# Moving a mixing stage's element work from GpSimd to VectorE, and a new order of its pieces

## The chip, the cores and the metric

The kernel runs on one core of one Trainium2 chip. The metric is the device time of one execution in microseconds (us). Five engines work in parallel, each through its own queue in a fixed order: TensorE (PE, matrix products and transposes), VectorE (DVE), ScalarE (ACT), GpSimd (POOL) and SyncE (SP, which here issues most transfers).

## The reference

Input `x` is 1024 tokens by 1024 features in float32. A first block (four attention branches, merge, output projection) is followed by a second one, and the change is in the second block's mixing. There `z = rms_norm(x) @ w_in` is split into columns for four mixers, whose outputs of 256 features each are joined and multiplied by `w_out`; an MLP and a gated projection follow.

```python
a, b = jnp.split(conf_ab, 2, axis=-1)             # conformer convolution
u = causal_depthwise_conv(a * sigmoid(b), w_dw)   # 31 taps
y_conf = silu(layer_norm(u, ln_g, ln_b)) @ w_pw

c = jnp.cumsum(log_sigmoid(f_logit), axis=1)      # forgetting attention, 4 heads of 64
logits = q @ k.T * scale + c_i - c_j              # causal mask, softmax, @ v

y_sc = sc_b * causal_depthwise_conv(sc_c * sc_h, w_sc)     # short convolution, 3 taps

# multiscale pool: mean of the last 2, 4, 8, 16 tokens, minus the token,
# a 64x64 product for each group, a scale

h = h + rms_norm(concat([y_conf, y_att, y_sc, y_pool]) @ w_out)
```

## The kernel before

All large products keep float32 accuracy by splitting each operand in a high part (rounded to the chip's fp32r type) and a low part (the rest), and by adding three products: high by high, high by low, low by high (`mm3`, lines 229 to 231). A product of 128 by 512 outputs over 1024 inputs is thus 24 matmuls. High parts are made by `copy` (line 147 on ScalarE, 149 on VectorE), low parts by `sub_lo`, which subtracts the high part from the value, on GpSimd (line 155) or on VectorE (line 157):

```python
if eng == "p":
    po.tensor_tensor(lo, x, hi.bitcast(F32), op=ALU.subtract)
else:
    ve.scalar_tensor_tensor(out=lo, in0=x, scalar=scale, in1=hi.bitcast(F32), ...)
```

Weights come from memory in pieces (`wr`) and are split into `wh` and `wl` by `split_w`. Which engine makes a low part is in the table `_T`: `WLO2` for the weights of the mixing stage, `CLO` for the conformer's output, a fixed pattern in `split_mix` for the mixers' outputs. In the kernel before, all of these are GpSimd's (`split_mix`: the first half of the tokens GpSimd's, the second VectorE's). GpSimd also adds the two halves of an attention tile's output in `join` (line 825, used in both blocks), computes the shift adds of the pooling (line 1512) and the power -1/2 of a normalization (line 1447).

The conformer's convolution has 31 taps for two groups of 128 channels (m = 0, 1) and two halves of 512 tokens. Each tap is one VectorE instruction (line 1332) that reads the input shifted by some tokens and adds it, times a weight, to an accumulator. The taps are Python generators in a list `convs`; `conv_steps(n)` lets n taps be written into the program. It is called with `CPP` = 2 after each large product (`product_done`), with `CS` after each attention tile, and to the end by the item `t`.

The order of the mixing stage is the string `WORK` in `_T`: each item is one piece of work, and a framework's list scheduler then orders the instructions of each engine by the program's order, dependences and buffers. `s0` and `s1` are the short convolution's channel groups with their products, `A` one query tile of the first pair of heads (eight), `B` one of the second pair, `q` the second pair's queries and keys, `p` the pooling, `c` one step of the conformer's finish (transposes, layer normalization, product), `w` the weights of the output projection, `0a` to `7` the splits of a mixer's output into parts (`split_mix`), `e` one early product of the output projection, `g` the gains, `t` the rest of the taps.

An attention tile: scores on TensorE (`s`, lines 795 to 799), maximum on VectorE (`Pm`, `mx`, line 836), exponential on ScalarE, scaling on VectorE (line 150), transposes on TensorE (`t`, line 274), their high parts on ScalarE and low parts on VectorE (`PT`), value matmuls (`o`, line 814), `join`.

Of the kernel before, what the change touches and what calls it, by code (L numbers as in the profile page):

```python
# [12 lines left out]
ALU = mybir.AluOpType  # L13
# [4 lines left out]
P = 128  # L18
# [6 lines left out]
SLOPES = [2.0 ** -2, 2.0 ** -4, 2.0 ** -6, 2.0 ** -8]  # L25
QS = 0.125

_T = dict(STA='s', XN1=0, PWT=1, PO='0x1', PO2={}, PS=2, PSX=0, PSE='a', PB=99, PEA=(0, 1, 4), WB=8, XL=3, CLO='p', STE=None, STW=None, ST1='b', ST2='b', PLP='pvv', WLO2='p', QXP=1, LW='vp', LEAD=10, FD={0: 'g', 1: 'b', 6: 'g'}, FW=(0, 2), AG=0, PREO=(0, 2, 1), PMB=0, PWB=1, PM=3, SG=2, FA={(0, 2): 'g', (0, 3): 'mmm', (0, 7): 'qm', (1, 0): 'gg', (1, 6): 'gz'}, FB={(0, 3): 'm', (0, 7): 'qm', (1, 3): 'm', (1, 5): 'z', (1, 7): 'm'}, FC={(0, 3): 'mm', (0, 7): 'q', (1, 3): 'zm', (1, 6): 'm'}, NORM='v', NORM2='v', CS=8, MM=2, SB=2, TB=3, OB=1, WHI='aaav', WLO='pv', PTH='a', NW=9, NBLK=31, PTB=2, XN=1, AS=(2, 4, 6, 7), CPP=2, CALT=1, WORK='s0 A A A A A A A A s1 q t B c B B c c B p w B 5 6b c c c 4 0a 1a g 6a 7 3a 2 e e c c c B e B c B 1b e 0b 3b', KS=(2, 0, 3, 1))


_C1 = [("trel", 1024), ("wrel", 640), ("crel", 256), ("brel", 128), ("brel2", 128), ("dm", 512), ("xi", 256), ("zeta", 256)]
# [45 lines left out]
def hybrid_then_mix_kernel(ctx: ExitStack, tc, I, c1, c2, out, dbg=None, upto=99):  # L77
# [162 lines left out]
    convs = []  # L240

    def conv_steps(n):
        for _ in range(n):
            if convs:
                if next(convs[0], "end") == "end":
                    convs.pop(0)
                elif _T["CALT"]:
                    convs.append(convs.pop(0))

    def product_done(last):  # L250
        conv_steps(_T["CPP"])
# [550 lines left out]
    def pv(dst, Pm, n, lo, v, start=True, stop=True):  # L802

        for c0 in range(0, n, 4):
            w = min(4, n - c0)
            tp = trb()
            for j in range(w):
                transpose(tp[:, j * P:(j + 1) * P], Pm[:, (c0 + j) * P:(c0 + j + 1) * P], ident)
            PT = cur[0].tile([P, 4, 2, P], F32R, name=nm("PT"), tag="PT", bufs=_T["PTB"])
            t3 = tp[:, :w * P].rearrange("p (j q) -> p j q", q=P)  # L810
            copy(PT[:, :w, 0, :], t3, pick("pt", _T["PTH"]))
            sub_lo(PT[:, :w, 1, :], t3, PT[:, :w, 0, :])
            for j in range(w):
                pe.matmul(dst, v(lo + c0 + j), PT[:, j].rearrange("p a q -> p (a q)"), start=start and c0 + j == 0,  # L814
                          stop=stop and c0 + j == n - 1, skip_group_check=True)

    def join(dst, o_):

        u = cur[0].tile([P, P], F32, name=nm("ju"), tag="ju", bufs=2)
        for hh in range(2):  # L820
            r = slice(hh * 64, hh * 64 + 64)
            oh = o_[:, hh * 256:hh * 256 + 256]
            copy(u[r, :], oh[64:128, :P], "a")
            ve.tensor_reduce(out=dst[r, :], in_=oh[0:64, :].rearrange("p (a q) -> p q a", a=2), op=ALU.add, axis=AX.X)  # L824
        po.tensor_tensor(dst, dst, u[:], op=ALU.add)  # L825
# [517 lines left out]
    for m in range(2):  # L1343
        u, w, evac = conf_group(m)
        us.append(u)
        first.append(w)
        conf_evac.append(evac)
        z_half(hT2, w, 0, evac)
        convs.append(conv(m, 0))
    assert not pend  # L1350
    uid[1] = 1
    ph.close()
# [9 lines left out]

    for m in range(2):
        z_half(hT2, first[m], 1, conf_evac[m])
        convs.append(conv(m, 1))
    qk0, w, evac = qk_group(0)
    z_group(hT2, w, evac)
    qk = [qk0]
# [54 lines left out]
    def conf_rest():  # L1423
        wp = W()
        raw = main.tile([P, 2, 256], F32, name=nm("wr"), tag="w", bufs=NW)
        hi, lo = [cur[0].tile([P, 2, 256], F32R, name=nm("wp"), tag="wp", bufs=2) for _ in range(2)]
        sy.dma_start(raw[:], kview(I["w_conf_pw_2"][0]))
        copy(hi[:], raw[:], "a")
        sub_lo(lo[:], raw[:], hi[:], "p")
        wp.hi = lambda k, c0, c1: hi[:, k, c0:c1]  # L1430
        wp.lo = lambda k, c0, c1: lo[:, k, c0:c1]
        sa = A(2)
        for half in range(2):
            sa.alloc(half, 0)
            vv = blk(F32, (P, 2, 512))
            for q in range(4):
# [12 lines left out]
                ve.tensor_scalar(xc[:], tp[:, :256], mv[:, 0:1], r[:, 0:1], op0=ALU.subtract, op1=ALU.mult)  # L1449
                tp = trb()  # L1450
                for m in range(2):
                    transpose(tp[:, m * P:(m + 1) * P], xc[:, m * P:(m + 1) * P], ident)
                for m in range(2):
                    ve.tensor_scalar(vv[:, m, q * P:(q + 1) * P], tp[:, m * P:(m + 1) * P], V["ln_g"][:, m:m + 1],
                                     V["ln_b"][:, m:m + 1], op0=ALU.mult, op1=ALU.add)
                yield
            for m in range(2):
                t = tmp("tz", 512)
                ac.activation(t[:], vv[:, m, :], AF.Tanh, scale=0.5)
                ve.scalar_tensor_tensor(out=vv[:, m, :], in0=t[:], scalar=1.0, in1=vv[:, m, :], op0=ALU.add, op1=ALU.mult)  # L1460
                copy(sa.hi(m, half), vv[:, m, :], "a")
                sub_lo(sa.lo(m, half), vv[:, m, :], sa.hi(m, half), _T["CLO"])
# [10 lines left out]
    def split_mix(k, halves=(0, 1)):  # L1473
        for half in halves:
            mix.alloc(half, k // 2)
            cs = slice(half * 512, (half + 1) * 512)
            copy(mix.hi(k, half), y32[k][:, cs], "a")
            sub_lo(mix.lo(k, half), y32[k][:, cs], mix.hi(k, half), "pv"[half])

    def short_conv(m):  # L1480
        if True:
# [16 lines left out]
    def pooling():  # L1498
# [7 lines left out]
        for m in range(2):  # L1506
# [5 lines left out]
                eng.tensor_tensor(dst[r, l:], src[r, :S - l], src[r, l:], op=ALU.add)  # L1512
                copy(dst[r, :l], src[r, :l], "v")
            s2 = blk()
            shift_add(po, s1, g, 1)
            if m == 0:
                lo_, hi_ = slice(0, 64), slice(64, 128)
                shift_add(po, s2, s1, 2, hi_)
                ve.tensor_copy(s2[lo_, :], s1[lo_, :])
                fin, fre = s2, s1  # L1520
            else:
                lo_, hi_ = slice(0, 64), slice(64, 128)
                shift_add(po, s2, s1, 2)
                shift_add(po, s1, s2, 4)
                shift_add(po, s2, s1, 8, hi_)
# [5 lines left out]
            ve.tensor_sub(fre[:, :16], fre[:, :16], g[:, :16])  # L1531
            for half in range(2):
# [17 lines left out]
    def out_early():  # L1550
        for t in range(NT // 2):
# [6 lines left out]
            ve.tensor_mul(early[t], m[:], gains[0][:, :512])  # L1558
            yield

    steps = dict(A=attention(0), B=attention(1), c=conf_rest(), e=out_early())
    works = dict(g=load_gains, s0=lambda: short_conv(0), s1=lambda: short_conv(1), t=lambda: conv_steps(140), q=second_qk, p=pooling)
    for c in steps:
        works[c] = lambda c=c: next(steps[c])
    for k in range(8):
# [514 lines left out]
```

## Time and profile before

| | us |
|---|---|
| median of 3 runs | 2347.11 (2343.71 to 2349.87) |
| the profiled execution | 2345.36 |
| its span in the profile | 2343.5 |
| TensorE busy | 2239.7 (96%) |
| VectorE busy | 1499.8 (64%) |
| ScalarE busy | 963.1 (41%) |
| GpSimd busy | 600.0 (26%) |

Mean granted clock of TensorE over the profiled execution: 0.983 of the full clock. The mixing stage lies between about 1185 and 1536 us of the span. A profile row names a line, an engine, an operation and tiles (output, an arrow, inputs), with buffer numbers left out; a number behind `x` counts instructions.

### The profile page before, as it was taken

How to read it: one execution, taken by the hardware profiler on the slowest of the kernel's cores; microseconds unless marked ns; L12 is line 12 of the kernel's file. 1: busy time of each engine (PE TensorE's matmuls, PEld its weight loads, DVE VectorE, ACT ScalarE, POOL GpSimd, SP SyncE). 2: the span in 40 equal slices, each digit the busy share in tenths (PEclk: the TensorE clock that was granted, in tenths of full speed). 3: DMA queues.
4: the chain of work that ended last, by engine and by line, in shares of the span. 5: the costliest groups of instructions: out<-in, count | busy, mean ns of one | idle time of the engine just before them, and what ended most of it. 6: DMA issues, size and time to landing. Idle time of an engine off the chain costs nothing. (4 is left out here: it accounts for less than half of the span.)

```text
span 2343.5 us, 30368 instructions
## 1 busy us (share of the span) xinstructions
PE 2239.7 (96%) x11004; PEld 1856.9 (79%) x11004; DVE 1499.8 (64%) x2849; ACT 963.1 (41%) x1937; POOL 600.0 (26%) x514
## 2 busy tenths in 40 slices
PE   7999999999989999999997997899999999999898
PEld 6788888888877778887876886677888878888787
DVE  7634456665667766534589766566567677677773
ACT  6211344444546544422312343534544453344442
POOL 4222110011265533324331125312133430000021
PEclk9999999999999999999998998999999999999999
DMA  9431211122132252224311110146555695534222
GB/s 327 153 95 58 64 63 55 45 91 63 41 122 86 82 155 81 86 81 153 109 42 50 46 59 28 46 171 211 174 180 189 198 357 194 177 108 156 95 74 90
DMA packets 202784, 272.73 MB, mean 116 GB/s; under 512 B 17086, under 2 KB 126214, under 8 KB 202634
## 3 DMA queue, kind: packets, MB, share of 16 engines
q1 hardware_dynamic: 194240, 257.95, 34.1%
q10 hardware_dynamic: 8394, 12.84, 1.8%
q8 instruction: 87, 1.43, 0.2%
q14 instruction: 63, 0.52, 0.1%
HBM read 199.43 MB, written 71.32 MB: 116 GB/s over the span
## 5 line engine op out<-in xcount | busy, mean ns | idle before, releaser
L229 PE MATMUL mm<-blk,wh 128*128 128x512 f32 x1264 | 506.1, 401 | 26.7 <-DVE blk L157 10.5
L230 PE MATMUL mm<-blk,wh 128*128 128x512 f32 x1264 | 502.2, 397 | 0.6 <-DVE blk L157 0.6
L231 PE MATMUL mm<-blk,wl 128*128 128x512 f32 x1264 | 500.8, 396 | 1.0 <-POOL wl L155 1.0
L229 PEld LDWEIGHTS mm<-blk,wh 128*128 128x128 f32 x1264 | 239.1, 189 | 80.6 <-issue 14.2
L231 PEld LDWEIGHTS mm<-blk,wl 128*128 128x128 f32 x1264 | 239.2, 189 | 50.7 <-POOL wl L155 1.4
L155 POOL TENSOR_TENSOR wl<-wr,wh 128x1024 fp32r<-128x1024 f32 (+2 forms) x70 | 172.0, 2457 | 412.3 <-ACT wh L147 192.5
L230 PEld LDWEIGHTS mm<-blk,wh 128*128 128x128 f32 x1264 | 239.6, 190 | 47.0 <-DVE blk L157 1.0
L229 PE MATMUL mm<-wh,blk 128*128 128x512 f32 (+3 forms) x544 | 196.9, 363 | 5.2 <-DVE fl L149 2.1
L231 PE MATMUL mm<-wh,blk 128*128 128x512 f32 (+3 forms) x544 | 193.6, 357 | 1.1 <-DVE blk L157 1.1
L157 DVE SCALAR_TENSOR_TENSOR wh<-blk,wh 128x1024 fp32r<-128x1024 f32 x116 | 138.3, 1221 | 71.6 <-issue 54.2
L147 ACT ACTIVATE wh<-blk 128x1024 fp32r<-128x1024 f32 x116 | 117.1, 1053 | 162.6 <-PE s L1991 75.7
L230 PE MATMUL mm<-wl,blk 128*128 128x512 f32 (+3 forms) x480 | 170.0, 355 | 5.7 <-DVE wl L157 5.0
L307 POOL TENSOR_TENSOR sm<-sm,mhalf 128x1 f32<-128x1 f32 x64 | 38.4, 603 | 444.7 <-DVE sm L306 427.7
L147 ACT ACTIVATE blk<-mm 64x512 fp32r<-64x512 f32 (+3 forms) x138 | 78.1, 569 | 160.4 <-PE mm L231 112.4
L157 DVE SCALAR_TENSOR_TENSOR PT<-t,PT 128x512 fp32r<-128x512 f32 (+3 forms) x224 | 111.3, 515 | 47.6 <-ACT PT L147 46.7
L147 ACT ACTIVATE PT<-t 128x512 fp32r<-128x512 f32 (+3 forms) x224 | 95.2, 460 | 110.7 <-PE o L814 70.4
L147 ACT ACTIVATE wh<-wr 128x1024 fp32r<-128x1024 f32 (+2 forms) x91 | 93.7, 1031 | 98.6 <-DMA wr<-in_w_in_dram 22.5
L229 PEld LDWEIGHTS mm<-wh,blk 128*128 128x128 f32 x544 | 103.4, 190 | 22.6 <-issue 2.3
L231 PEld LDWEIGHTS mm<-wh,blk 128*128 128x128 f32 x544 | 103.4, 190 | 16.9 <-DVE blk L157 1.9
L230 PEld LDWEIGHTS mm<-wl,blk 128*128 128x128 f32 x480 | 91.7, 191 | 19.3 <-DVE wl L157 6.5
L825 POOL TENSOR_TENSOR blk<-blk,ju 128x128 f32<-128x128 f32 x64 | 34.5, 538 | 278.9 <-DVE blk L824 278.8
L1332 DVE SCALAR_TENSOR_TENSOR blk<-blk,dwc,blk 128x512 f32<-128x512 f32 (+23 forms) x124 | 102.6, 878 | 0.4
(364 smaller groups left out, 4912.5 us busy)
## 6 DMA issues: line engine op xcount, KB each, us to landing
acc<-acc SPq DMA_DIRECT2D x96, 256.0 KB, 2.6
wr<-in_w_merge_dram SPq DMA_DIRECT2D x32, 512.0 KB, 4.0
wu<-in_w_up_dram SPq DMA_DIRECT2D x32, 512.0 KB, 5.4
blk<-in_w_down_dram SPq DMA_DIRECT2D x32, 512.0 KB, 7.1
blk<-ss SPq DMA_DIRECT2D x32, 512.0 KB, 3.5
wr<-in_w_in_dram SPq DMA_DIRECT2D x27, 512.0 KB, 4.2
ss<-us SPq DMA_DIRECT2D x48, 256.0 KB, 2.3
blk<-sa SPq DMA_DIRECT2D x24, 512.0 KB, 3.3
```

The source lines that it names most:

```text
L147: return ac.activation(dst, src, AF.Copy, scale=1.0 if scale is None else scale)
L155: po.tensor_tensor(lo, x, hi.bitcast(F32), op=ALU.subtract)
L157: ve.scalar_tensor_tensor(out=lo, in0=x, scalar=scale, in1=hi.bitcast(F32), op0=ALU.mult, op1=ALU.subtract)
L229: pe.matmul(dst, sh, mh, start=(i == 0), stop=False)
L230: pe.matmul(dst, sh, ml, start=False, stop=False)
L231: last = pe.matmul(dst, sl, mh, start=False, stop=(i == n - 1))
L307: po.tensor_tensor(dst, dst, mhalf[:, :m], op=ALU.pow)
L825: po.tensor_tensor(dst, dst, u[:], op=ALU.add)
L1332: ve.scalar_tensor_tensor(out=acc[:, c:c1], in0=u[:, c - l:c1 - l], scalar=w, in1=acc[:, c:c1], op0=ALU.mult, op1=ALU.add)
```

## The change

Low parts of the mixing stage's weights (`WLO2`), of the conformer's output (`CLO`), of its last weight `wp` and of the mixers' outputs go to VectorE, as do the pooling's shift adds and `join`'s add (the last in both blocks). The taps take the two channel groups in turn within one half of the tokens and then the second half; the calls that write them stand in `tc.issue_after`, named after the last matmul of a product or attention tile. The conformer's finish normalizes tile q before it transposes back tile q - 1. The pooling's grouped products become an item of their own (`P`), and `WORK` is new: the pooling and its products of z come ahead of `s1`, the conformer's first half (taps `t`, steps `c`) between the first `B` tiles, its second half (`u`) later.

```diff
-_T = dict(... CLO='p', ... WLO2='p', ... CS=8, ... WORK='s0 A A A A A A A A s1 q t B c B B c c B p w B 5 6b c c c 4 0a 1a g 6a 7 3a 2 e e c c c B e B c B 1b e 0b 3b', ...)
+_T = dict(... CLO='v', ... WLO2='v', ... CS=4, CSB=8, ... WORK='s0 A A A A A A A A p s1 q t c B c B c B c B c 0a 1a P w 5 4 6 7 g 2 3a e u c B e c B c e B c c e B 1b 0b 3b', ...)
...
             if convs:
-                if next(convs[0], "end") == "end":
-                    convs.pop(0)
-                elif _T["CALT"]:
-                    convs.append(convs.pop(0))
+                half, steps_ = convs.pop(0)
+                if next(steps_, "end") != "end":
+                    convs.insert(sum(h == half for h, _ in convs), (half, steps_))
...
     def product_done(last):
-        conv_steps(_T["CPP"])
+        with tc.issue_after(last.ins):
+            conv_steps(_T["CPP"])
...
-                pe.matmul(dst, v(lo + c0 + j), PT[:, j].rearrange("p a q -> p (a q)"), start=start and c0 + j == 0,
+                behind_pe[0] = pe.matmul(dst, v(lo + c0 + j), PT[:, j].rearrange("p a q -> p (a q)"),
...
-        po.tensor_tensor(dst, dst, u[:], op=ALU.add)
+        ve.tensor_tensor(dst, dst, u[:], op=ALU.add)
...
-        sub_lo(lo[:], raw[:], hi[:], "p")
+        sub_lo(lo[:], raw[:], hi[:])
...
+            held = None
+            for q in range(4):
+                xc = normed(q)
+                if held is not None:
+                    turned(q - 1, held)
+                held = xc
                 yield
+            turned(3, held)
...
-            sub_lo(mix.lo(k, half), y32[k][:, cs], mix.hi(k, half), "pv"[half])
+            sub_lo(mix.lo(k, half), y32[k][:, cs], mix.hi(k, half))
...
-            shift_add(po, s1, g, 1)
+            shift_add(ve, s1, g, 1)
...
-        conv_steps(_T["CS"] if n[0] in "A" else 0)
+        if n[0] in "AB":
+            with tc.issue_after(behind_pe[0].ins):
+                conv_steps({"A": _T["CS"], "B": _T["CSB"]}[n[0]])
```

Two places of the order. VectorE's queue near the end of the taps, before (`blk` with two `blk` inputs and `dwc` is a tap, `fl` the forget logits):

```order
L149 CAST wh_11967<-wr_11961 128x1024
L1332 SCALAR_TENSOR_TENSOR blk_11224<-blk_11312,dwc,blk_11224 128x482
L1332 SCALAR_TENSOR_TENSOR blk_11223<-blk_11225,dwc,blk_11223 128x512
L1332 SCALAR_TENSOR_TENSOR blk_11224<-blk_11312,dwc,blk_11224 128x512
L157 SCALAR_TENSOR_TENSOR blk_11676<-mm_11898,blk_11676 128x4x64
L149 COPY fl<-mm_11898 128x4
L1332 SCALAR_TENSOR_TENSOR blk_11223<-blk_11225,dwc,blk_11223 128x512
L1332 SCALAR_TENSOR_TENSOR blk_11224<-blk_11312,dwc,blk_11224 128x512
L1378 TENSOR_TENSOR fl<-fl,bf 128x32
```

And with the change, at the same place:

```order
L1334 SCALAR_TENSOR_TENSOR blk_11223<-blk_11225,dwc,blk_11223 128x512
L1334 SCALAR_TENSOR_TENSOR blk_11224<-blk_11312,dwc,blk_11224 128x512
L157 SCALAR_TENSOR_TENSOR blk_11676<-mm_11898,blk_11676 128x4x64
L149 COPY fl<-mm_11898 128x4
L157 SCALAR_TENSOR_TENSOR wl_11968<-wr_11961,wh_11967 128x1024
L1334 SCALAR_TENSOR_TENSOR blk_11224<-blk_11312,dwc,blk_11224 128x482
L157 SCALAR_TENSOR_TENSOR wl_11972<-wr_11964,wh_11971 128x1024
L1334 SCALAR_TENSOR_TENSOR blk_11223<-blk_11225,dwc,blk_11223 128x512
L1334 SCALAR_TENSOR_TENSOR blk_11224<-blk_11312,dwc,blk_11224 128x512
L1380 TENSOR_TENSOR fl<-fl,bf 128x32
L157 SCALAR_TENSOR_TENSOR wl_12090<-wr_12087,wh_12089 128x1024
```

Three low parts `wl` of 1024 columns have come into the queue between the taps. The taps themselves stand where they stood, ahead of the first attention tile.

TensorE's queue behind the last product of the second pair's queries and keys, before (`mm` with `wh` and `wl` is a large product; `t` are transposes, `s` scores):

```order
L231 MATMUL mm_13041<-blk_11055,wl_12943 128x512
L274 MATMUL t_13138<-c_63,blk_11223 128x128
L274 MATMUL t_13138<-c_63,blk_11224 128x128
L229 MATMUL mm_13356<-blk_10677,wh_13348 128x512
L230 MATMUL mm_13356<-blk_10678,wh_13348 128x512
L231 MATMUL mm_13356<-blk_10677,wl_13349 128x512
L229 MATMUL mm_13356<-blk_10677,wh_13348 128x512
L795 MATMUL s_13203<-blk_12926,blk_12924 128x384
L797 MATMUL s_13203<-blk_12928,blk_12924 128x384
L799 MATMUL s_13203<-causR,identR 128x128
```

And with the change:

```order
L231 MATMUL mm_13164<-blk_11055,wl_13066 128x512
L276 MATMUL t_13246<-c_63,Pm_13225 128x128
L276 MATMUL t_13252<-c_63,Pm_13231 128x128
L276 MATMUL t_13272<-c_63,blk_11223 128x128
L276 MATMUL t_13272<-c_63,blk_11224 128x128
L797 MATMUL s_13362<-blk_13049,blk_13047 128x384
L799 MATMUL s_13362<-blk_13051,blk_13047 128x384
L801 MATMUL s_13362<-causR,identR 128x128
L797 MATMUL s_13368<-blk_13050,blk_13048 128x384
L799 MATMUL s_13368<-blk_13052,blk_13048 128x384
L801 MATMUL s_13368<-causR,identR 128x128
```

Before, the pooling's products of z stand between the tiles here. With the change these stand earlier, and behind the last product of q and k come only tiles' scores, transposes and value matmuls, with the conformer's small products, up to the first early product of the output projection.

## Rows read from the trace of the kernel before

**Rows 1.** The page's first part: busy time of each engine over the span (instructions behind x).

```profile
PE 2239.7 (96%) x11004; PEld 1856.9 (79%) x11004; DVE 1499.8 (64%) x2849; ACT 963.1 (41%) x1937; POOL 600.0 (26%) x514
```

**Rows 2.** Windows of the three stretches; columns named in the first line.

```profile
core 0: us, PE busy (x) PEld busy (x) DVE busy (x) ACT busy (x) POOL busy (x), PEclk, DMA share, GB/s
1185.00:1302.00 117.00, 99.49 (x506) 84.36 (x505) 112.36 (x165) 22.72 (x39) 25.11 (x13) 0.93 0.14 37
1302.00:1413.00 111.00, 110.73 (x574) 92.38 (x573) 75.02 (x172) 48.27 (x108) 30.01 (x21) 1.00 0.20 57
1413.00:1536.00 123.00, 102.00 (x463) 80.01 (x462) 74.09 (x184) 53.14 (x114) 46.51 (x38) 0.88 0.13 39
```

**Rows 3.** TensorE's waits, 1185 to 1302: waited for, us in all, times, longest.

```profile
PE mm L229 <- DVE fl L149: 8.0, 2, 5.9
PE mm L229 <- DVE blk L157: 6.2, 1, 6.2
```

**Rows 4.** A window at low granted clock, columns as in rows 2.

```profile
1449.00:1466.00 17.00, 12.33 (x44) 10.22 (x43) 14.30 (x38) 4.84 (x13) 6.90 (x5) 0.51 0.01 1
```

**Rows 5.** VectorE's groups by shape, 1185 to 1302, and line 1332 (ns min/median/max).

```profile
L1332 DVE SCALAR_TENSOR_TENSOR blk<-blk,dwc,blk 128x512 f32<-128x512 f32 x57 | 46.2, 844 | 0.0
...
L1332 DVE SCALAR_TENSOR_TENSOR blk<-blk,dwc,blk 128x505 f32<-128x505 f32 x2 | 3.6, 1815 | 0.0
...
L1332 DVE SCALAR_TENSOR_TENSOR blk<-blk,dwc,blk 128x492 f32<-128x492 f32 x2 | 2.5, 1249 | 0.0
...
L149 DVE CAST wh<-wr 128x520 fp32r<-128x520 f32 x1 | 0.4, 420 | 0.0
...
L1332 DVE SCALAR_TENSOR_TENSOR blk<-blk,dwc,blk x117: 705/737/2891, 1189.3 to 1301.5; 128x512 f32<-128x512 f32 x57, 128x511 f32<-128x511 f32 x2, 128x510 f32<-128x510 f32 x2, 128x509 f32<-128x509 f32 x2
```

**Rows 6.** Timeline of VectorE, of GpSimd beside it, of VectorE later (start, us).

```profile
1207.64 5.69 DVE L1332 SCALAR_TENSOR_TENSOR blk<-blk,dwc,blk 128x505 f32<-128x505 f32 x2
...
1205.15 7.64 POOL L155 TENSOR_TENSOR wl<-wr,wh 128x1024 fp32r<-128x1024 f32 x2 [6.01 <-issue]
...
1285.58 3.11 DVE L1332 SCALAR_TENSOR_TENSOR blk<-blk,dwc,blk 128x512 f32<-128x512 f32 x2
```

**Rows 7.** GpSimd's groups by shape, 1185 to 1302.

```profile
L155 POOL TENSOR_TENSOR wl<-wr,wh 128x1024 fp32r<-128x1024 f32 x5 | 15.8, 3170 | 31.4 <-DVE wh L149 25.3 <-issue 6.0
L155 POOL TENSOR_TENSOR wl<-wr,wh 128x520 fp32r<-128x520 f32 x4 | 6.0, 1504 | 35.2 <-DMA wr<-in_w_in_dram 27.5 <-DVE wh L149 7.5
```

**Rows 8.** VectorE's groups by shape, 1185 to 1536.

```profile
L157 DVE SCALAR_TENSOR_TENSOR PT<-t,PT 128x512 fp32r<-128x512 f32 x24 | 16.3, 685 | 8.4 <-ACT PT L147 8.3
...
L157 DVE SCALAR_TENSOR_TENSOR blk<-blk,blk 128x512 fp32r<-128x512 f32 x8 | 6.3, 791 | 5.5 <-ACT blk L147 5.5
...
L1528 DVE SCALAR_TENSOR_TENSOR blk<-blk,c,blk 128x1008 f32<-128x1008 f32 x2 | 2.5, 1263 | 0.0
...
L157 DVE SCALAR_TENSOR_TENSOR wl<-wr,wh 128x1024 fp32r<-128x1024 f32 x2 | 2.4, 1223 | 0.1
...
L836 DVE CUSTOM_DVE_ANT_0 Pm<-s,xb 128x128 f32<-128x128 f32 x8 | 2.3, 288 | 4.8 <-DMA xb<-cF_d 3.4 <-PE s L799 1.4
```

**Rows 9.** Windows of the pooling's products and the early ones, as in rows 2.

```profile
1414.40:1436.00 21.60, 21.54 (x109) 18.13 (x109) 13.09 (x38) 6.91 (x20) 5.76 (x5) 1.00 0.08 25
1490.00:1531.00 41.00, 36.19 (x190) 28.67 (x188) 25.83 (x58) 22.00 (x45) 6.58 (x7) 1.00 0.17 52
```

**Rows 10.** VectorE's waits, 1413 to 1536, columns as in rows 3.

```profile
DVE sm L856 <- ACT Pm L848: 7.6, 6, 2.4
DVE Pm L836 <- PE t L274: 7.0, 4, 5.4
...
DVE xc L1449 <- POOL sm L1447: 5.9, 4, 3.2
```

**Rows 11.** GpSimd's instructions on the tile `ju` (ns min/median/max).

```profile
L825 POOL TENSOR_TENSOR blk<-blk,ju x64: 451/460/1952, 304.0 to 1533.3; 128x128 f32<-128x128 f32 x64
```

**Rows 12.** Window in the first block, columns as in rows 2.

```profile
600.00:800.00 200.00, 185.93 (x1058) 158.55 (x1057) 142.21 (x205) 107.48 (x239) 111.73 (x125) 0.98 0.30 94
```

More of the change, by code (lines that the diff above doesn't have):

```diff
@@ L26 @@
 QS = 0.125
-_T = dict(STA='s', XN1=0, PWT=1, PO='0x1', PO2={}, PS=2, PSX=0, PSE='a', PB=99, PEA=(0, 1, 4), WB=8, XL=3, CLO='p', STE=None, STW=None, ST1='b', ST2='b', PLP='pvv', WLO2='p', QXP=1, LW='vp', LEAD=10, FD={0: 'g', 1: 'b', 6: 'g'}, FW=(0, 2), AG=0, PREO=(0, 2, 1), PMB=0, PWB=1, PM=3, SG=2, FA={(0, 2): 'g', (0, 3): 'mmm', (0, 7): 'qm', (1, 0): 'gg', (1, 6): 'gz'}, FB={(0, 3): 'm', (0, 7): 'qm', (1, 3): 'm', (1, 5): 'z', (1, 7): 'm'}, FC={(0, 3): 'mm', (0, 7): 'q', (1, 3): 'zm', (1, 6): 'm'}, NORM='v', NORM2='v', CS=8, MM=2, SB=2, TB=3, OB=1, WHI='aaav', WLO='pv', PTH='a', NW=9, NBLK=31, PTB=2, XN=1, AS=(2, 4, 6, 7), CPP=2, CALT=1, WORK='s0 A A A A A A A A s1 q t B c B B c c B p w B 5 6b c c c 4 0a 1a g 6a 7 3a 2 e e c c c B e B c B 1b e 0b 3b', KS=(2, 0, 3, 1))
+_T = dict(STA='s', XN1=0, PWT=1, PO='0x1', PO2={}, PS=2, PSX=0, PSE='a', PB=99, PEA=(0, 1, 4), WB=8, XL=3, CLO='v', STE=None, STW=None, ST1='b', ST2='b', PLP='pvv', WLO2='v', QXP=1, LW='vp', LEAD=10, FD={0: 'g', 1: 'b', 6: 'g'}, FW=(0, 2), AG=0, PREO=(0, 2, 1), PMB=0, PWB=1, PM=3, SG=2, FA={(0, 2): 'g', (0, 3): 'mmm', (0, 7): 'qm', (1, 0): 'gg', (1, 6): 'gz'}, FB={(0, 3): 'm', (0, 7): 'qm', (1, 3): 'm', (1, 5): 'z', (1, 7): 'm'}, FC={(0, 3): 'mm', (0, 7): 'q', (1, 3): 'zm', (1, 6): 'm'}, NORM='v', NORM2='v', CS=4, CSB=8, MM=2, SB=2, TB=3, OB=1, WHI='aaav', WLO='pv', PTH='a', NW=9, NBLK=31, PTB=2, XN=1, AS=(2, 4, 6, 7), CPP=2, CALT=1, WORK='s0 A A A A A A A A p s1 q t c B c B c B c B c 0a 1a P w 5 4 6 7 g 2 3a e u c B e c B c e B c c e B 1b 0b 3b', KS=(2, 0, 3, 1))
 _C1 = [("trel", 1024), ("wrel", 640), ("crel", 256), ("brel", 128), ("brel2", 128), ("dm", 512), ("xi", 256), ("zeta", 256)]
@@ L244, in conv_steps @@
             if convs:
-                if next(convs[0], "end") == "end":
-                    convs.pop(0)
-                elif _T["CALT"]:
-                    convs.append(convs.pop(0))
+                half, steps_ = convs.pop(0)
+                if next(steps_, "end") != "end":
+                    convs.insert(sum(h == half for h, _ in convs), (half, steps_))
+    behind_pe = [None]
     def product_done(last):
-        conv_steps(_T["CPP"])
+        with tc.issue_after(last.ins):
+            conv_steps(_T["CPP"])
         due = []
@@ L813, in pv @@
             for j in range(w):
-                pe.matmul(dst, v(lo + c0 + j), PT[:, j].rearrange("p a q -> p (a q)"), start=start and c0 + j == 0,
-                          stop=stop and c0 + j == n - 1, skip_group_check=True)
+                behind_pe[0] = pe.matmul(dst, v(lo + c0 + j), PT[:, j].rearrange("p a q -> p (a q)"),
+                                         start=start and c0 + j == 0, stop=stop and c0 + j == n - 1, skip_group_check=True)
     def join(dst, o_):
@@ L1348, in hybrid_then_mix_kernel @@
         z_half(hT2, w, 0, evac)
-        convs.append(conv(m, 0))
+        convs.append((0, conv(m, 0)))
     assert not pend
@@ L1364, in hybrid_then_mix_kernel @@
         z_half(hT2, first[m], 1, conf_evac[m])
-        convs.append(conv(m, 1))
+        convs.append((1, conv(m, 1)))
     qk0, w, evac = qk_group(0)
@@ L1435, in conf_rest, with normed @@
             vv = blk(F32, (P, 2, 512))
-            for q in range(4):
+            def normed(q):
                 t = 4 * half + q
@@ L1449, in conf_rest, with turned @@
                 ve.tensor_scalar(xc[:], tp[:, :256], mv[:, 0:1], r[:, 0:1], op0=ALU.subtract, op1=ALU.mult)
+                return xc
+            def turned(q, xc):
                 tp = trb()
@@ L1514, in pooling @@
             s2 = blk()
-            shift_add(po, s1, g, 1)
+            shift_add(ve, s1, g, 1)
             if m == 0:
                 lo_, hi_ = slice(0, 64), slice(64, 128)
-                shift_add(po, s2, s1, 2, hi_)
+                shift_add(ve, s2, s1, 2, hi_)
                 ve.tensor_copy(s2[lo_, :], s1[lo_, :])
@@ L1522, in pooling @@
                 lo_, hi_ = slice(0, 64), slice(64, 128)
-                shift_add(po, s2, s1, 2)
-                shift_add(po, s1, s2, 4)
-                shift_add(po, s2, s1, 8, hi_)
+                shift_add(ve, s2, s1, 2)
+                shift_add(ve, s1, s2, 4)
+                shift_add(ve, s2, s1, 8, hi_)
                 ve.tensor_copy(s2[lo_, :], s1[lo_, :])
@@ L1531, in pooling, with pool_out @@
             ve.tensor_sub(fre[:, :16], fre[:, :16], g[:, :16])
+            pooled.append((bd, fre, fin))
+    pooled = []
+    def pool_out():
+        for m, (bd, fre, fin) in enumerate(pooled):
             for half in range(2):
@@ L1559, in out_early, with conv_rest @@
             yield
+    def conv_rest(half):
+        while any(h <= half for h, _ in convs):
+            conv_steps(1)
     steps = dict(A=attention(0), B=attention(1), c=conf_rest(), e=out_early())
-    works = dict(g=load_gains, s0=lambda: short_conv(0), s1=lambda: short_conv(1), t=lambda: conv_steps(140), q=second_qk, p=pooling)
+    works = dict(g=load_gains, s0=lambda: short_conv(0), s1=lambda: short_conv(1), t=lambda: conv_rest(0), u=lambda: conv_rest(1), P=lambda: pool_out(), q=second_qk, p=pooling)
     for c in steps:
```

## The prediction

> **What bounds the kernel.** I read the page's first part, then windows over the mixing stage, then what TensorE waits for in each, then single instructions. TensorE is busy for 96% of the span [rows 1], so time can only come from the idle 4% or from stretches at a lower granted clock, and the mixing stage holds a large part of both. I cut it in three [rows 2]. The first stretch, 117 us, ends where the taps end: VectorE is busy 112.4 us of it (96%) and TensorE 99.5, so VectorE sets the pace. In the second, 111 us (second convolution, first-pair tiles A, second-pair q and k), TensorE is busy 110.7 us at full clock. In the third, 123 us (second-pair tiles B, the conformer's finish, the early products), it is busy 102.0 us, at a mean granted clock of 0.88. In the first stretch TensorE waits for VectorE almost alone [rows 3]: 5.9 us at once for the evacuation of the forget logits (`fl`), 6.2 us for a low part. With such gaps the granted clock falls to the 1.2 GHz level, as from 1449 to 1466, where it is 0.51 [rows 4].
>
> **What the moves return on VectorE.** In the first stretch 57 taps of 512 columns have a mean of 844 ns, while the median of all 117 taps is 737 [rows 5]: 57 x 0.107 = 6.1 us too much. Two pairs of other lengths are stretched like that of 505 columns (2 x 1.08 = 2.2 us each), three like that of 492 (2 x 0.51 = 1.0 each). Together 13.5 us. The timeline shows the cause [rows 6]: two taps take 5.69 us instead of 1.47 just while GpSimd runs two `wl` low parts in 7.64. Low parts on GpSimd cost VectorE time; without them I let all 13.5 us go.
>
> **What they add there.** Five `wl` of 1024 columns and four of 520 [rows 7] now run on VectorE. Its own prices are 1.223 us for 1024 columns and 0.685 for 512 [rows 8]: 5 x 1.22 + 4 x 0.69 = 8.9 us. By the order two long and four short ones (5.2 us) stand ahead of the `fl` evacuation, three long ones behind it. Of the 13.5 us, 1.6 lie behind it (two taps in 3.11 us [rows 6]), so it comes 11.9 - 5.2 = 6.7 us earlier. **First stretch: -7 us.** Bounds: if nothing of the stretching goes, +5 us; if both groups of waits on VectorE go whole, -14. I take the middle of the gain, since VectorE is still over 90% busy there. A new wait could come with it: a low part in VectorE's queue waits for the weight's transfer, with taps queued behind it. GpSimd stood idle 27.5 us for that before its short low parts [rows 7], the far bound; but VectorE's own copy of such a weight, in the same place of its queue, waited 0.0 [rows 5]. I take 0.
>
> **What the ties do.** Nothing, by the order: they bind instructions of the engine on which the named instruction runs, which is TensorE, and taps run on VectorE. All of them still stand ahead of the first A tile, as before. The new alternation (both channel groups inside half 0, then half 1) leaves each duration as it was.
>
> **The second stretch.** The pooling's four products of z (96 matmuls) come forward from the third stretch to a place under the A tiles. In the third they took 21.6 us with TensorE busy throughout [rows 9]. Here TensorE has no idle time to lend: +22 here, -22 there, net 0. VectorE gains the six shift adds of the pooling (1.26 us each by the nearest row, 1008 columns [rows 8], 7.6 us), about six `wl` (7.3 us) and the pooling's scaling: with them it is busy some 95 of 133 us, still less than TensorE. I cost them at nothing; without that cover they are 15 us. The transfers of the pooling's weights pass those of q in SP's queue; DMA is busy 0.20 of this stretch [rows 2], so 0.
>
> **The third stretch.** Without the pooling's products 123 - 22 = 101 us are left. Now nothing of 24 matmuls stands behind q and k: up to the first early product the order has score, transpose and value matmuls of five B tiles, the conformer's half 0 and four small grouped products. On TensorE these are 131 matmuls, about 16 us at full clock by their columns (21.6 / 96 = 0.225 us for 512). On VectorE the 106 instructions between q's last low part and the last one that the early products need come to 43.9 us by the unstretched durations of their shapes: low parts of blocks 9.5, of PT 5.2, score maxima 8.3, scaling 4.8, conformer 10.4, reductions and joins 4.0, small ones 1.7. So VectorE sets the pace here. Its use in the nearest stretch of before, 1449 to 1466, with no product either, was 14.3 of 17.0 us, 84% [rows 4]: 43.9 / 0.84 = 52 us; the first low part of the early products stands 7 us sooner, so I take 50. The conformer's transposes of one tile now behind the normalizing of the next spare waits on GpSimd's power (5.9 us before [rows 10]); that lies inside the 84%. Then come the early products with tiles B5 to B7: 219 matmuls, 35 us at full clock by their columns; from 1490 to 1531 TensorE was 88% busy [rows 9], and small matmuls cost more than their columns: 46 us. Sum 96 against 101. **Third stretch: -5 us.** Bounds: VectorE at 100% and a covered tail, 44 + 40 = 84, -17; VectorE at the third stretch's mean use, 74.1 / 123 = 60% [rows 2], 73 + 46 = 119, +18.
>
> **The joins of the first block.** 48 adds of 128x128 go from GpSimd (median 460 ns [rows 11]) to VectorE, where no row has the shape: 0 to 22 us in all. In the least covered stretch there TensorE is 93% and VectorE 71% busy [rows 12]. I take 0, nearest to the lower end since TensorE covers them; without that cover, up to 22.
>
> **Sum.** -7 + 0 - 5 + 0 = -12 us against the profiled execution (2345.36 us, span 2343.5): 2333.4, so 2333. The median of the runs stands 1.75 us above the profiled one, well under the 0.3% (7 us) that a measurement of this kernel can tell.
>
> **The rivals.** (1) *Uncovered second-pair tiles.* From the end of q to the first early product nothing long stands on TensorE. For it: VectorE's waits in the third stretch are for ScalarE's exponentials and TensorE's transposes [rows 10], one chain through three engines, and an idle TensorE falls to 0.5 clock [rows 4]. Against it: two or three tiles and a conformer group are under way at once. It decides once VectorE's use there falls under 70% (63 us). At 60%: +18 - 7 = +11, 2356 us.
>
> (2) *All idle time and half clock of the stage goes:* -10 in the first stretch, -17 in the third: 2318. Against it: VectorE has more to do in all three.
>
> (3) *The first stretch's gain is given back.* The A tiles start sooner, but their first maxima wait for the forget bias that goes through DRAM (3.4 us [rows 8]) and the end of q stays where it was. Only about half of the third's gain is left: 2343.
>
> (4) *The moves cost what they add and return nothing.* If the stretching had another cause, the first stretch would be +5 us, and the third, its low parts at 791 ns instead of 685 [rows 8], 44 x 1.15 / 0.84 = 60 instead of 52, +3: 2353. The taps of rows 6 speak against it. A rule of the Trainium skill speaks for it (Perfetto Trace Analysis, section Optimizing Scalar/DVE Operations): where VectorE is saturated, giving some of its work to GpSimd may pay; the change takes work from GpSimd in just the stretch where VectorE is 96% busy. The same section adds that the two share a read port, so that it might not help; by that half, the trace agrees.
>
> **How the numbers follow.** Forecast 0.50 (its own range 2325 to 2341), (1) 0.19, (2) 0.11, (3) 0.15, (4) 0.05. Faster by over 0.3% (under 2340): 0.46 of the forecast and (2), 0.57. Slower (over 2354): 0.14 of (1) and 0.02 of (4), 0.16. Within: the other 0.27. The range 2319 to 2355 leaves out half of (1), half of (2) and the tail of (4).
>
> **What would show it.** In the profile after: taps near 740 ns without stretched pairs; TensorE's wait for `fl` under 2 us and the taps done about 5 us sooner; no gap of TensorE from the first A tile to the end of q, which comes about 15 us later than before; then some 50 us with VectorE over 80% busy and TensorE half idle, part of it at 0.5 clock; a first block as long as before. I am wrong if that stretch takes over 63 us, or if the taps stay as long as they were.

## The result and the profile after

Over 7 runs each, the changed kernel takes 2336.25 us (2332.15 to 2339.66) and the kernel before 2348.13 (2343.71 to 2351.46): a ratio of 0.9948, 95% interval 0.9933 to 0.9963, or 12 us less. The profiled execution took 2339.66 us, with a span of 2337.8. That is only 5.7 us under the profiled one of before, because its span lost 8.1 us ahead of the mixing stage: 3.7 in the first 400 matmuls and 3.7 in a piece of the first block that comes back below. So I compare stretches, not spans.

The first part of the page of the changed kernel:

```profile
PE 2239.1 (96%) x11004; PEld 1854.8 (79%) x11004; DVE 1519.8 (65%) x2952; ACT 963.0 (41%) x1937; POOL 491.1 (21%) x411
```

GpSimd lost 109 us of work, and VectorE has only 20 more [rows 1]. The windows of [rows 2], by the same work, follow. They begin some 8 us later in the span; the second ends with the second pair's queries and keys; the third is split at the first early product and ends at the place in the work where 1536 lay before. Columns as there:

```profile
1193.00:1310.00 117.00, 107.02 (x542) 90.63 (x541) 111.58 (x180) 24.64 (x41) 3.30 (x4) 0.94 0.16 42
1310.00:1434.00 124.00, 119.73 (x614) 99.92 (x612) 86.51 (x206) 49.91 (x110) 2.45 (x3) 1.00 0.18 53
1434.00:1468.50 34.50, 27.07 (x122) 18.34 (x122) 33.09 (x105) 21.91 (x53) 3.25 (x5) 0.90 0.06 16
1468.50:1528.60 60.10, 53.83 (x266) 43.02 (x267) 37.78 (x86) 28.07 (x58) 5.88 (x4) 0.97 0.21 70
```

In the first, TensorE gets through 542 matmuls in 117 us, against 506. VectorE's groups in that window and TensorE's waits there answer to [rows 5], [rows 7] and [rows 3]:

```profile
L1334 DVE SCALAR_TENSOR_TENSOR blk<-blk,dwc,blk 128x512 f32<-128x512 f32 x60 | 42.7, 746 | 0.3
...
L157 DVE SCALAR_TENSOR_TENSOR wl<-wr,wh 128x1024 fp32r<-128x1024 f32 x6 | 7.3, 1220 | 0.0
...
L157 DVE SCALAR_TENSOR_TENSOR wl<-wr,wh 128x520 fp32r<-128x520 f32 x4 | 2.8, 688 | 0.0
...
L1334 DVE SCALAR_TENSOR_TENSOR blk<-blk,dwc,blk 128x505 f32<-128x505 f32 x2 | 1.5, 737 | 0.0
```

```profile
PE mm L230 <- DVE wl L157: 4.4, 2, 2.9
PE mm L229 <- DVE fl L149: 1.6, 1, 1.6
PE mm L229 <- DVE blk L157: 1.3, 2, 1.1
```

Taps have a mean of 746 ns instead of 844, the stretched pairs are gone (505 columns: 737 instead of 1815), the low parts cost what their prices said. The waits for `fl` and for the low part `blk` fell from 14.2 us to 2.9, and a new one of 4.4 us came, for the short low parts `wl`.

To follow a stretch through all kernels I take four marks with the same work between them in each: the first matmul of the first block's output projection, the first maximum of an A tile, the end of the last low part of the second pair's queries and keys, and the last matmul of the second block's output projection. In the timeline of the kernel before (start and duration, us) they are:

```profile
1070.37 0.39 PE L229 MATMUL mm<-wh,blk 128*128 128x512 f32 x1
...
1307.45 0.29 DVE L836 CUSTOM_DVE_ANT_0 Pm<-s,xb 128x128 f32<-128x128 f32 x1 [2.37 <-DMA xb<-cF_d]
...
1413.09 0.69 DVE L157 SCALAR_TENSOR_TENSOR blk<-mm,blk 64x512 fp32r<-64x512 f32 x1 [0.66 <-ACT blk L147]
...
1595.53 0.39 PE L231 MATMUL mm<-wh,blk 128*128 128x512 f32 x1
```

and in that of the changed kernel:

```profile
1078.46 0.39 PE L229 MATMUL mm<-wh,blk 128*128 128x512 f32 x1
...
1310.77 0.29 DVE L838 CUSTOM_DVE_ANT_0 Pm<-s,xb 128x128 f32<-128x128 f32 x1 [1.26 <-DMA xb<-cF_d]
...
1434.13 0.69 DVE L157 SCALAR_TENSOR_TENSOR blk<-mm,blk 64x512 fp32r<-64x512 f32 x1
...
1588.12 0.39 PE L231 MATMUL mm<-wh,blk 128*128 128x512 f32 x1
```

The third mark is the end of its row (1413.78 and 1434.82), the others are starts. The pooling's products lie in the third part before and in the second after; otherwise only tiles and conformer steps cross a mark. All parts are in us of one profiled execution each, the ratio is that of the timed runs; "first block" is the time from the 3600th to the 4800th matmul.

| kernel | first | second | third | sum | first block | ratio to before (95%) |
|---|---|---|---|---|---|---|
| before | 237.1 | 106.3 | 181.7 | 525.2 | 254.6 | 1 |
| changed | 232.3 | 124.1 | 153.3 | 509.7 | 258.3 | 0.9948 (0.9933 to 0.9963) |
| e1, low parts alone | 229.3 | 107.6 | 181.8 | 518.8 | 253.0 | 0.9975 (0.9965 to 0.9985) |
| e2, order alone | 236.8 | 127.6 | 151.5 | 515.9 | 253.7 | 0.9956 (0.9942 to 0.9970) |
| e3, joins back | 228.7 | 129.6 | 152.4 | 510.7 | 254.8 | 0.9948 (0.9934 to 0.9961) |
| e4, joins alone | 237.4 | 106.2 | 180.3 | 523.9 | 256.9 | 1.0008 (0.9998 to 1.0017) |
| e5, late taps tied | 227.2 | 138.9 | 153.6 | 519.6 | 256.9 | 0.9988 (0.9978 to 0.9999) |
| e6, pooling behind q | 232.4 | 104.6 | 176.2 | 513.2 | 255.3 | 0.9969 (0.9959 to 0.9980) |
| e7, GpSimd reads | 241.5 | 123.3 | 153.0 | 517.9 | 257.3 | one run |
| e8, GpSimd writes | 232.0 | 122.9 | 152.8 | 507.7 | 256.0 | one run |
| e9, first joins back | 229.0 | 128.4 | 154.1 | 511.5 | 255.2 | 0.9935 (0.9920 to 0.9950) |
| e10, no interleaving | 232.0 | 123.3 | 162.7 | 518.0 | 256.4 | 0.9996 (0.9985 to 1.0006) |
| e11, old order | 232.2 | 105.8 | 181.9 | 519.9 | 256.1 | 0.9981 (0.9969 to 0.9993) |
| e12, taps tied | 230.5 | 148.1 | 151.1 | 529.7 | 253.1 | 1.0026 (1.0016 to 1.0036) |

The changed kernel and e8, with the same VectorE order, differ by 2.0 us in the sum; so much I take as scatter.

### The profile page after: what moved, and what is told of

Same layout as the page of the kernel before. It is cut to its first block, busy times and chain, and to the rows that moved or that the text cites. A ratio compares the mean times of both kernels' runs of the same rounds, so it can differ in the third digit from the quotient of the medians.

```text
span 2337.8 us, 30294 instructions
## 1 busy us (share of the span) xinstructions
PE 2239.1 (96%) x11004; PEld 1854.8 (79%) x11004; DVE 1519.8 (65%) x2952; ACT 963.0 (41%) x1937; POOL 491.1 (21%) x411
## 4 chain that ended last, share of the span: by engine, by line
PE 46%; DVE 6%; DMA 2%; ACT 1%; issue 1%; POOL 0%; SPq 0%; DVEq 0%; POOLq 0%; ACTq 0%
PE mm L230 6%; PE mm L231 6%; PE mm L229 6%; DVE blk L1334 2%; PE s L1674 2%; PE s L1676 2%; PE s L1675 2%; PE t L276 1%; PE t L2014 1%; PE t L2015 1%; PE t L2016 1%; PE s L2015 1%; PE mm L2015 1%; PE s L2016 1%; PE mm L2016 1%; PE t L1674 1%
## 5 line engine op out<-in xcount | busy, mean ns | idle before, releaser
L155 POOL TENSOR_TENSOR wl<-wr,wh 128x1024 fp32r<-128x1024 f32 (+1 forms) x50 | 122.6, 2453 | 479.7 <-ACT wh L147 281.3
L157 DVE SCALAR_TENSOR_TENSOR wl<-wr,wh 128x1024 fp32r<-128x1024 f32 (+2 forms) x69 | 88.2, 1279 | 30.8 <-PE mm L230 14.0
L1150 POOL TENSOR_TENSOR acc<-tz,acc 128x512 f32<-128x512 f32 x48 | 68.8, 1436 | 132.0 <-DVE tz L1149 91.4
## 6 DMA issues: line engine op xcount, KB each, us to landing
acc<-acc SPq DMA_DIRECT2D x96, 256.0 KB, 2.7
ss<-us SPq DMA_DIRECT2D x48, 256.0 KB, 2.2
```

The source lines that it names most:

```text
L1150: po.tensor_tensor(acc[:], t[:], acc[:], op=ALU.add)
```

## The experiments

**Moves and order apart.** e1 is the kernel before with only the low parts moved:

```diff
-CLO='p', ... WLO2='p'
+CLO='v', ... WLO2='v'
...
-        sub_lo(lo[:], raw[:], hi[:], "p")
+        sub_lo(lo[:], raw[:], hi[:])
...
-            sub_lo(mix.lo(k, half), y32[k][:, cs], mix.hi(k, half), "pv"[half])
+            sub_lo(mix.lo(k, half), y32[k][:, cs], mix.hi(k, half))
```

> The kernel before with all low parts of the mixing stage (weights of that stage, the conformer's output and last weight, the mixers' outputs) on VectorE; pooling's shift adds, joins and the old order kept. Theory (GpSimd's low parts stretch VectorE's taps): the 57 taps of 512 columns fall from a mean of 844 ns to about 740, the evacuation of the forget logits comes 7 to 9 us sooner within the stage, as in the changed kernel, and the time is 2336 to 2342 us, 6 to 12 under the kernel before. Rival (the gain is the new order's; the moved work only loads VectorE): taps shorten, but the stage gives it back later, 2346 to 2352 us.

The first part falls by 7.8 us, the sum by 6.4; the `fl` evacuation comes 10.3 us sooner from the first mark (205.0 against 215.3). All of the gain arises before the first A tile, and only 1.4 us is lost again. VectorE's group of taps and TensorE's wait for `fl` in e1's first stretch:

```profile
L1332 DVE SCALAR_TENSOR_TENSOR blk<-blk,dwc,blk 128x512 f32<-128x512 f32 x59 | 42.0, 742 | 0.2
```

```profile
PE mm L229 <- DVE fl L149: 1.6, 1, 1.6
```

The theory holds, at the small end: the median was 2342.3, just over its range and 6.3 under the 2348.61 of the kernel before, timed beside it.

e2 is the changed kernel with low parts, shift adds and joins given back to GpSimd:

```diff
-CLO='v', ... WLO2='v'
+CLO='p', ... WLO2='p'
...
-            shift_add(ve, s1, g, 1)
+            shift_add(po, s1, g, 1)
...
-        ve.tensor_tensor(dst, dst, u[:], op=ALU.add)
+        po.tensor_tensor(dst, dst, u[:], op=ALU.add)
```

> The changed kernel with GpSimd's work given back (low parts, shift adds, joins), so the new order alone. Theory: the first stretch is as slow as before (taps at a mean of about 840 ns, a wait of about 6 us for the forget logits), the third keeps part of its gain: 2340 to 2347 us. Rival (the order makes the gain): 2333 to 2338 us.

The first part stays (236.8), with the old group of taps and the old wait, as VectorE's groups and TensorE's waits of e2 show:

```profile
L1334 DVE SCALAR_TENSOR_TENSOR blk<-blk,dwc,blk 128x512 f32<-128x512 f32 x59 | 47.7, 842 | 0.1
```

```profile
PE mm L229 <- DVE fl L149: 8.0, 2, 5.9
```

But the sum falls by 9.3 us. The median, 2339.31, lies between the theory's range and the rival's: the order gives more than the theory allowed, but not the whole gain. Moves and order add up: 6.4 + 9.3 = 15.7, and the change has 15.5. The order, which here includes the interleaving of the conformer's finish, is the larger half, which I had not forecast.

**What stretches the taps.** To the changed kernel e7 adds useless GpSimd subtractions while the taps run, e8 useless memsets:

```diff
+    scr = cur[0].tile([P, 512], F32, name="scr", tag="scr", bufs=1)
+    for k_ in range(12):
+        po.tensor_tensor(scr[:], us[k_ % 2][:, 0:512], us[k_ % 2][:, 0:512], op=ALU.subtract)
```

```diff
+    scr = cur[0].tile([P, 512], F32, name="scr", tag="scr", bufs=1)
+    po.tensor_tensor(scr[:, 0:1], us[1][:, 0:1], us[1][:, 0:1], op=ALU.subtract)
+    for k_ in range(24):
+        po.memset(scr[:], 0.0)
```

> The changed kernel plus 12 useless GpSimd subtractions of 128x512, both inputs in on-chip memory, into a scratch tile, while the taps run; VectorE's order unchanged. Theory (a GpSimd operation that reads stretches taps): tap mean from 746 to 800 ns or more, single taps of over 1.5 us beside those subtractions, fl 3 to 9 us later. Rival (the taps of the kernel before were stretched by something else, such as waits for weights): tap mean under 755.

> The changed kernel plus 24 useless GpSimd memsets of 128x512 into a scratch tile, which read nothing, while the taps run; VectorE's order unchanged. Theory (only reads stretch taps): tap mean under 755 ns, fl within 1 us of the changed kernel. Rival (any GpSimd work does): tap mean over 790.

The timeline of e7, VectorE and then GpSimd:

```profile
1214.84 9.55 DVE L1334 SCALAR_TENSOR_TENSOR blk<-blk,dwc,blk 128x509 f32<-128x509 f32 x7
...
1208.41 15.43 POOL L1370 TENSOR_TENSOR scr<-blk 128x512 f32<-128x512 f32 x11
```

and of e8:

```profile
1202.91 4.66 DVE L1334 SCALAR_TENSOR_TENSOR blk<-blk,dwc,blk 128x509 f32<-128x509 f32 x7
...
1201.11 14.13 POOL L1371 MEMSET scr<- 128x512 f32 x24
```

VectorE executes the same instructions in the same order in both and in the changed kernel. The same seven taps take 9.55 us beside reading GpSimd operations and 4.66 beside writing ones. In e7 the `fl` evacuation comes 216.3 us from the first mark, 10.0 later than in the changed kernel and about where it was before; in e8 it stays at 206.3. One number of e7's theory missed: the subtractions fell beside taps of 499 to 511 columns, so the mean of the 512-column taps stayed at 746 ns; the mean over all 120 taps of the convolution rose from 737 to 816, and in e8 it is 735. Together the two runs settle what stretched the taps of the first stretch. The Trainium skill (SBUF — State Buffer, section Who interferes with whom) states this rule: a VectorE instruction with two inputs in on-chip memory contends with a GpSimd instruction that reads it, not with one that only writes. Both runs agree.

**The joins.** e3 and e4 move the one line of `join` in either kernel:

```diff
-        ve.tensor_tensor(dst, dst, u[:], op=ALU.add)
+        po.tensor_tensor(dst, dst, u[:], op=ALU.add)
```

> The changed kernel with only the joins' adds back on GpSimd. Theory (the first block covers them): the first block as long, 2334 to 2338 us. Rival (the 4.5 us by which the profiled first block of the changed kernel was longer, between its 3600th and 4800th matmul, are the joins on VectorE): that piece is shorter by 4 to 5 us again, 2330 to 2333 us.

> The kernel before with only the joins' adds on VectorE. Theory (covered): 2346 to 2350 us, each piece of the first block as long as before. Rival (joins cost): the piece between the 3600th and 4800th matmul longer by 4 to 5 us, 2351 to 2354 us.

The piece of the first block is 253.0 to 255.2 us in the six traces with its joins on GpSimd (mean 254.1) and 255.3 to 258.3 in the eight with them on VectorE (mean 256.7). So they cost 2.6 us: the cover was not whole, and the rival's 4 to 5 us were too much. The timed runs don't resolve it: e3's ratio is that of the change, e4's 1.0008 with an interval that holds 1. On VectorE such an add takes a median of 292 ns, and up to 1830, as the row on the tile `ju` in the changed kernel has it (ns min/median/max):

```profile
L827 DVE TENSOR_TENSOR blk<-blk,ju x64: 257/292/1830, 307.3 to 1511.7; 128x128 f32<-128x128 f32 x64
```

e9 keeps joins on VectorE in the mixing stage only:

```diff
-        ve.tensor_tensor(dst, dst, u[:], op=ALU.add)
+        (ve if uid[1] else po).tensor_tensor(dst, dst, u[:], op=ALU.add)
```

> The changed kernel with the joins of the first block on GpSimd and those of the mixing stage on VectorE. Theory (ten traces: the piece of the first block from the 3600th to the 4800th matmul takes 254.0 us on average with joins on GpSimd, 256.8 with them on VectorE): that piece falls to 254, the mixing stage stays at 510, and the time is 2331 to 2336 us, about 3 under the changed kernel. Rival (chance differences of the piece): 2336 us, piece at 256 to 258.

The piece falls to 255.2, the mixing stage stays within the scatter (511.5), the median is 2332.76. It is faster than the kernel before and has the lowest ratio of all, 0.9935 (0.9920 to 0.9950); whether it beats the changed kernel (0.9948) stays open, as the intervals overlap.

Moving the joins also changes VectorE's order behind the first block, since the list scheduler plans anew. With the first block's joins on GpSimd the first part is 228.7 us in e3 and 229.0 in e9, against 232.3 in the changed kernel; the second part takes it back (129.6 and 128.4 against 124.1). So a first part that is 3 us shorter need not shorten the stage.

**What in the order makes the gain.** e6 puts the pooling back behind q:

```diff
-WORK='s0 A A A A A A A A p s1 q t c B ...
+WORK='s0 A A A A A A A A s1 q p t c B ...
```

> The changed kernel with the pooling and its products of z back behind q and k, the rest of the new order kept. Theory (moving them nets nothing, plus 22 in one stretch and minus 22 in the other; what counts is the order of conformer steps and tiles): mixing stage within 3 us of the changed kernel's 509.7, 2334 to 2339 us. Rival (they were worth more as cover of the B tiles): 2 to 8 us faster, 2328 to 2334; third (their place under the A tiles makes the gain): 4 to 9 us slower, 2340 to 2345.

Second and third part are 104.6 and 176.2: their sum is 3.4 us over the changed kernel's, and the stage 3.5. The theory of a net of nothing misses, by a little; the place under the A tiles is worth about 3 us, little more than the scatter of 2.0. The median, 2339.68, lies between the theory's range and the third one's.

e10 takes the interleaving out of the conformer's finish:

```diff
-                xc = normed(q)
-                if held is not None:
-                    turned(q - 1, held)
-                held = xc
+                turned(q, normed(q))
                 yield
-            turned(3, held)
```

> The changed kernel with the conformer's finish as before: each tile is normalized and turned back in the same step, with GpSimd's power in between. Theory (the gain of the third stretch comes from the order of pieces; the interleaving was costed inside VectorE's use): mixing stage 509 to 513 us, time 2335 to 2340. Rival (the interleaving hides GpSimd's power, up to 6 us of waits): mixing stage 513 to 518, time 2339 to 2345.

The rival holds in the stage: the sum grows by 8.3 us, through the third part. The median, 2346.79, is beyond even the rival's range. TensorE's waits there in e10:

```profile
PE t L276 <- DVE xc L1451: 7.1, 4, 2.4
PE o L816 <- DVE PT L157: 6.3, 6, 2.7
```

and in the changed kernel:

```profile
PE o L816 <- DVE PT L157: 2.7, 5, 1.3
...
PE t L276 <- DVE xc L1451: 0.7, 2, 0.4
```

Without the interleaving TensorE's transposes wait 7.1 us for the normalized tile `xc`; the value matmuls behind them wait longer too. The tile stands at the end of a chain, from its statistics on VectorE over GpSimd's power back to VectorE. VectorE's own idle time before `xc` in e10 is short, as its group from 1434 to 1540 shows:

```profile
L1451 DVE TENSOR_SCALAR xc<-t,cmv,sm 128x256 f32<-128x256 f32 x6 | 3.2, 542 | 0.8 <-POOL sm L1449 0.6
```

So it is the whole chain, with VectorE's other work in between, that TensorE waits for, and not the power alone.

e11 is the changed kernel with the old order of pieces:

```diff
-WORK='s0 A A A A A A A A p s1 q t c B c B c B c B c 0a 1a P w 5 4 ...
+WORK='s0 A A A A A A A A s1 q t u B c B B c c B p P w B 5 6b c c c ...
```

> The changed kernel with the old order of pieces (the rest of the taps whole behind q, the pooling's products right behind its sums). Theory (moves 6 to 8 us, order 9): first stretch as in the changed kernel, third as before, mixing stage 517 to 521 us, 2343 to 2348 us with 3 us lost in the first block's joins. Rival (moves and order need each other, the joins and shift adds being too much for VectorE without the new order): 522 us or more, 2347 to 2352.

First part as in the change, third as before, sum 519.9, as the theory said. Against e1 (518.8) it has the interleaving, the shift adds and the joins besides, and gains nothing by them beyond the scatter. With the interleaving the order gives 10.2 us (e11 to the changed kernel). Without it, e10 is only 0.8 us under e1, though e10 has the shift adds and joins on VectorE as well. So interleaving and order seem to need each other; no run takes the interleaving alone out of the old order. The kernel before, which has neither, fits: from 1413 to 1536 none of TensorE's waits is for `xc`.

**Ties that bind.** The `issue_after` calls of the change, ties for short, name a TensorE instruction, and by the order they leave VectorE's queue as it is; two kernels tie taps to VectorE instructions instead. In e5 the taps written after the last three A tiles stand behind the low part `PT` of the tile five before:

```diff
-            with tc.issue_after(behind_pe[0].ins):
+            tied.append(behind_ve[0])
+            if n[0] in "A" and len(tied) > 5:
+                with tc.issue_after(tied[-1 - 5].ins):
+                    conv_steps({"A": _T["CS"], "B": _T["CSB"]}[n[0]])
+            else:
                 conv_steps({"A": _T["CS"], "B": _T["CSB"]}[n[0]])
```

> The changed kernel with a tie that does bind taps: the taps written after the sixth, seventh and eighth A tile stand, on VectorE, behind the low part of the tile five before. Ten taps move from ahead of the first A tile to behind it, 7.4 us of VectorE's work. Theory (taps crowd the first stretch, VectorE has room under the A tiles): first A maximum 3 to 7 us sooner, 2330 to 2336 us. Rival (the taps ahead of it are only filler, and TensorE's end of q is set by TensorE): 2335 to 2339 us, the same as the changed kernel.

In e12 (on e9) all taps written after the weights of the attention values stand behind the last `wl` of those. That is the low part of the new 4.4 us wait, and the changed kernel's timeline shows what it waits behind:

```profile
1249.94 2.70 DVE L1334 SCALAR_TENSOR_TENSOR blk<-blk,dwc,blk 128x512 f32<-128x512 f32 x4
1252.55 0.69 DVE L157 SCALAR_TENSOR_TENSOR wl<-wr,wh 128x520 fp32r<-128x520 f32 x1
...
1253.88 2.67 DVE L1334 SCALAR_TENSOR_TENSOR blk<-blk,dwc,blk 128x512 f32<-128x512 f32 x4
1256.48 0.68 DVE L157 SCALAR_TENSOR_TENSOR wl<-wr,wh 128x520 fp32r<-128x520 f32 x1
```

Each short low part stands behind four taps.

```diff
-        with tc.issue_after(last.ins):
+        with tc.issue_after((v_lo[0] or last).ins):
             conv_steps(_T["CPP"])
...
+    v_lo[0] = last_lo[0]
...
-            with tc.issue_after(behind_pe[0].ins):
+            with tc.issue_after((v_lo[0] or behind_pe[0]).ins):
```

> The kernel of e9 (joins of the first block on GpSimd) with a tie that binds taps on VectorE: all taps written after the attention values' weights stand behind the low part of the last of those weights, for which TensorE waited 4.4 us behind taps in the changed kernel. 48 taps (35 us) move behind it; 30 still stand later than the last fl evacuation's former place. Theory (in the first stretch TensorE waits for VectorE work that stands behind taps): the 4.4 us and the 1.6 us for fl go, the first A maximum comes 4 to 8 us sooner, the mixing stage falls to 504 to 508 us, 2327 to 2333 us. Rival (VectorE's work before the first A tile is the same, only in another order, so the wait moves to the A tiles): wait gone but mixing stage 509 to 516 us, 2332 to 2339 us.

In e5 the first part shrinks as its theory said (227.2 against 232.3). In e12 the wait for the low part is gone, as TensorE's waits from 1180 to 1310 show, so it was the taps that stood in its way:

```profile
PE mm L233 <- DVE wl L159: 0.6, 1, 0.6
```

But its first part does not shrink (230.5 against 229.0 in e9), and both sums grow, by 9.9 us over the changed kernel and by 18.2 over e9: 519.6 and 529.7. Both theories miss, and both kernels come out slower than their rivals said (2344.67 and 2353.85). e12's waits of TensorE from 1295 to 1335, the first A tiles:

```profile
PE t L278 <- DVE Pm L150: 10.8, 3, 3.9
PE s L799 <- DVE mx L840: 10.4, 6, 4.4
```

In e12 36 of the 124 taps run behind the first A maximum, against 6 in e9. Many of them stand between a tile's maximum and its scaling, and TensorE waits for both.

## Why the prediction was right, and which of its steps were not

The forecast was 2333 us, 12 under the kernel before; the measured change is 12, and 2336.25 lies in the range. The steps did less well than the sum, which came out so close partly by luck.

**The first stretch: mechanism right, size about right.** Forecast -7 us. The `fl` evacuation came 9.0 us sooner (forecast 6.7), the first A tile 4.8 (taps done "about 5 us sooner"), and under the old order the low parts alone gave 7.8 there and 6.4 over the stage. The return of 13.5 us and the prices of the moved low parts held. One step failed: the new wait, which I took at 0 because the copy of such a weight had waited for no transfer. It is 4.4 us, and by the timeline and by e12, which is down to 0.6, it is for taps in front of the low part and not for a transfer.

**The ties do nothing.** All taps still ran ahead of the first A tile but the four of the short convolution. That they do nothing rests on the order, as no run takes them out alone; the two ties that bind cost 10 and 18 us.

**The second and third stretch: right in sum by parts that were wrong.** Forecast +22 and -27, measured +17.8 and -28.4. Of the net -10.6, against -5, the pooling's place, costed at nothing, is some 3 us. In the third, I forecast 50 us to the first early product and 46 behind it; they took 34.5 and 60.1. The first piece had VectorE 96% busy, not 84%, and TensorE 78%, not half idle; the early products began before all the VectorE work that I had put ahead of them was done; the rest of the tiles then ran among those products. The step that was wrong most is the interleaving, which I put "inside the 84%": by e10 it is worth 8.3 us, more than the gain I gave the whole stretch.

**The joins: mis-sized.** Forecast 0, measured 2.6 us over 14 traces: the cover that was to hide them did not hold. Over the whole, -15.5 in the stage and +2.6 in the first block make -12.9. The second and third stretch gained 5.6 us more than forecast, the first 2.2 less, and the joins cost 2.6: these errors nearly cancelled, which is luck.

**The rivals.** (1) fell: VectorE was 96% busy behind q, and TensorE's clock 0.90 there. (2) went too far: TensorE still waits, and the stage gained 15.5 of its 27. (3) fell, as the stage kept the gain; in e1 1.4 of 7.8 us went back. (4) fell to e1 and e7: the stretching was GpSimd's.

## What to carry to other kernels

Before low parts or adds are given to a half-idle GpSimd, look at VectorE's instructions beside them in the timeline: if one form has two durations, what GpSimd does there is paid on VectorE, and with VectorE as the pace it is paid in time. Judge a change of several parts by marks in the trace with the same work between them: here parts of +17.8, -28.4 and +2.6 us were plain in single profiles, while the timed runs could hardly tell 3 us. And a piece that shortens a chain (the interleaving) can be worth 8 us under one order and, as far as the runs here tell, nothing under another, so try it under the order that exposes the chain.

## What was not expected of the hardware

While GpSimd read without a break, VectorE's taps went at GpSimd's pace: in e7 one tap took 9.55 / 7 = 1.36 us while one GpSimd subtraction took 15.43 / 11 = 1.40, as if the two took turns. Before, the stretched taps lasted 2.4 to 2.9 us [rows 5] beside `wl` subtractions of 1024 columns, which took 2.7 to 2.8 each but for the first, with 4.8; beside those of 520 columns, which took 1.5 [rows 7], three lasted 1.8 and one 1.0. So over three lengths of GpSimd's instruction, and taps that are nearly alike, the loss goes with GpSimd's length. One tap of e7 does not fit: it lasted 3.0 us at the start of the subtractions, beside none longer than 1.4, and its cause stays open. A GpSimd memset of the same shape cost the taps nothing (4.66 / 7 = 0.67 us each).
